# Which engine waits for the last landings: from SyncE to GpSimd, without GpSimd's drain

## The chip, the cores and the metric

The kernel runs on one core of one Trainium2 chip. The time is device microseconds of one execution. A core has five engines that work side by side, each with its own queue of instructions: TensorE (PE in the profile), VectorE (DVE), ScalarE (ACT), GpSimd (POOL) and SyncE (SP). They meet only through semaphores: an instruction can wait until a semaphore has a value, and can step one when it is done. Transfers are issued from an engine's queue, run on 16 DMA engines, and step a semaphore by 16 in all when they have landed.

## The reference

Eight experts, each a layer of two matrix products with a ReLU between them, on its own 256 rows:

```python
# x: 8 x 256 x 512, w1: 8 x 512 x 2048, w2: 8 x 2048 x 512, all float32
h = np.matmul(x, w1)
h = np.maximum(h, 0)
return np.matmul(h, w2).astype(np.float32)
```

## The kernel before

The weights make up most of the bytes. They are loaded from GpSimd's queue (`load_w1`, `load_w2`, lines 130 to 139), which turns float32 into bfloat16 on the way, into two buffers each, one for even and one for odd experts. The first half of `x` comes by SyncE's queue as float32 and is cast by VectorE and ScalarE, the second half by GpSimd's queue. TensorE transposes `x` by an identity matrix, then works through the experts in pairs: the first layer of both experts of a pair (line 269), then the second layer of both (line 289). VectorE takes one half of each result out of PSUM and ScalarE the other (`layers`, lines 202 to 226), with the ReLU behind the first layer (lines 216 and 218) and as a plain copy into `o_sb` behind the second (line 225).

The output leaves in three stores. GpSimd, when it has issued its last loads and the first four experts are copied, stores these (line 165, semaphore `s_out[0]`). SyncE stores experts 4 to 6 (line 125, `s_out[1]`) and, when the last copy is done, expert 7 (line 127, `s_out[2]`). GpSimd's queue carries the loads and its store in the order of their issue, so that store moves behind the last weights. Everything that GpSimd has to do for the kernel is issued by line 165; behind it stands a drain (line 166), an instruction that ends when the engine has finished what was given to it. SyncE's list is a long row of waits that hand landings on to TensorE, then the two stores, and at the end of the program, at line 300, the waits for all three stores:

```python
    for s in s_out:
        sp.wait_ge(s, 16)
```

The framework's own closing is taken early (`tc.close()`, line 97), so the kernel ends in these waits, and behind them in whatever every program on this chip has behind its last instruction.

Of the kernel before, what the change touches and what calls it, by code (L numbers as in the profile page):

```python
# [9 lines left out]
def kernel(  # L10
# [73 lines left out]
    sp, pool, act, dve, pe = nc.sync, nc.gpsimd, nc.scalar, nc.vector, nc.tensor  # L84
# [78 lines left out]
            load_w2(e + b)  # L163
    copied(pool, G)
    pool.dma_start(out_r[:, :G], o_sb[:, :G]).then_inc(s_out[0], 16)
    pool.drain()

# [127 lines left out]
                        ins.then_inc((s_ob, s_oa)[m], 1)  # L297

    for s in s_out:
        sp.wait_ge(s, 16)  # L300


# [28 lines left out]
```

## Time and profile before

| | |
|---|---|
| time, median of 3 runs | 179.96 us (179.84 to 180.02) |
| the profiled execution, its own time | 179.85 us |
| its span, first to last instruction of the program | 178.5 us |
| TensorE busy | 130.2 us, 73% of the span |
| VectorE, ScalarE busy | 37.2 and 37.8 us |
| GpSimd busy | 12.6 us |
| GpSimd's DMA queue (q0) | 36.70 MB, 94.2% of the 16 engines' time |
| the hardware queue (q1) | 4.19 MB, 6.0% |
| mean granted TensorE clock | 0.963 |

How to read it: the profile is of one execution. The span counts only the program's own instructions; the time of an execution is longer, since something lies around them. Waiting, branching and issuing are not counted as busy time, so SyncE, which does nothing else, has no row among the busy engines; its waits have a view of their own. A drain counts as a sequencer instruction too and shows only in the view of its line. In the DMA issues, the last column is the time from issue to landing. In the lines of the timeline, the columns are start and duration in us, engine, line, operation, what it writes and reads, and in brackets the idle time before it with what ended that. A trailing q on an engine's name (SPq, POOLq) means its sequencer.

### The profile page before, as it was taken

What the parts mean: (1) busy time and instruction counts of PE and PEld (TensorE: products, weight loads), DVE (VectorE), ACT (ScalarE), POOL (GpSimd) and SP (SyncE); (2) the same over time, 40 slices, a digit from 0 to 9 for tenths busy, and PEclk for the clock granted to TensorE, in tenths of its full rate; (3) what the DMA queues carried; (4) which work ended last, traced back from release to release, by engine and by line L of the source; (5) the groups of instructions that cost most, each with busy time, mean ns of one, the idle gap of its engine ahead of it and who ended that gap; (6) DMA issues with size and microseconds to landing.
All of it is one profiled execution on the core that took longest, in us unless ns stands there. A gap on an engine that the chain in (4) does not pass through costs nothing. (4 is left out here: it accounts for less than half of the span.)

```text
span 178.5 us, 2361 instructions
## 1 busy us (share of the span) xinstructions
PE 130.2 (73%) x824; PEld 89.1 (50%) x832; DVE 37.2 (21%) x48; ACT 37.8 (21%) x49; POOL 12.6 (7%) x26
## 2 busy tenths in 40 slices
PE   0235299796949697899769398969496695998950
PEld 0224189693413296785333287954142694953410
DVE  0333673331010133131101033320101141311010
ACT  2464763221010122121100022220101121311010
POOL 3600000101010101001000101010201200000000
PEclk9999999999987999699999789999999999999996
DMA  5999999989989989999999998999998999999998
GB/s 195 350 218 235 217 195 235 224 191 231 231 191 224 235 191 220 235 202 209 235 209 202 235 224 187 235 228 195 224 235 191 220 235 194 207 224 209 269 423 353
DMA packets 4384, 40.90 MB, mean 229 GB/s; under 512 B 416, under 2 KB 416, under 8 KB 2208
## 3 DMA queue, kind: packets, MB, share of 16 engines
q0 software_dynamic: 3264, 36.70, 94.2%
q1 hardware_dynamic: 1120, 4.19, 6.0%
HBM read 71.30 MB, written 4.19 MB: 423 GB/s over the span
## 5 line engine op out<-in xcount | busy, mean ns | idle before, releaser
L269 PE MATMUL pt_h<-xe,w_sb 128*128 x512 | 65.4, 285 | 13.7 <-PEq L87 13.6
L269 PEld LDWEIGHTS pt_h<-xe,w_sb 128*128 x512 | 57.6, 147 | 22.0 <-issue 20.0
L289 PE MATMUL pt_o<-w_sb,ht_sb 128*128 x248 | 57.8, 387 | 11.8 <-PEq L87 11.4
L289 PEld LDWEIGHTS pt_o<-w_sb,ht_sb 128*128 x256 | 24.9, 99 | 43.4 <-issue 15.9
L218 DVE TENSOR_SCALAR ht_sb<-pt_h 128x512 bf16<-128x512 f32 x32 | 22.1, 692 | 52.9 <-PE pt_h L269 52.9
L216 ACT ACTIVATE ht_sb<-pt_h 128x512 bf16<-128x512 f32 x32 | 19.1, 597 | 57.9 <-PE pt_h L269 57.9
L253 PE MATMUL pt_tr<-identity,x_b 128*128 128x128 bf16 x64 | 7.5, 310 | 16.4 <-PEq L87 16.4
L225 DVE COPY out_sb<-pt_o 128x512 f32 x8 | 5.5, 692 | 66.5 <-PE pt_o L289 66.5
L225 ACT COPY out_sb<-pt_o 128x512 f32 x8 | 4.7, 586 | 64.6 <-PE pt_o L289 64.6
L253 PEld LDWEIGHTS pt_tr<-identity,x_b 128*128 128x128 bf16 x64 | 6.5, 144 | 17.1 <-issue 17.1
L131 POOL DMA_DIRECT2D w_sb<-in_w_dram x8 | 4.3, 534 | 70.9 <-ACTq L220 70.9
L195 DVE COPY xe<-pt_tr 128x1024 bf16<-128x1024 bf16 x2 | 4.9, 2454 | 5.2 <-PE pt_tr L253 5.2
L195 ACT COPY xe<-pt_tr 128x1024 bf16<-128x1024 bf16 x2 | 4.9, 2469 | 4.1 <-PE pt_tr L253 4.1
L136 POOL DMA_DIRECT2D w_sb<-in_w_dram x6 | 3.2, 536 | 35.5 <-ACT out_sb L225 35.5
L176 ACT CAST x_b<-x_f 128x1024 bf16<-128x1024 f32 x2 | 4.0, 2008 | 1.3 <-DMA x_f<-in_x_dram 1.3
L176 DVE CAST x_b<-x_f 128x1024 bf16<-128x1024 f32 x2 | 2.2, 1079 | 6.0 <-DMA x_f<-in_x_dram 6.0
L192 ACT COPY xe<-pt_tr 128x1024 bf16<-128x1024 bf16 x2 | 2.0, 1012 | 4.1 <-PE pt_tr L253 4.1
L192 DVE COPY xe<-pt_tr 128x1024 bf16<-128x1024 bf16 x2 | 1.4, 692 | 4.8 <-PE pt_tr L253 4.8
L138 POOL DMA_DIRECT2D w_sb<-in_w_dram x2 | 1.1, 531 | 17.1 <-ACT out_sb L225 17.1
L176 ACT COPY x_b<-x_c 128x1024 bf16<-128x1024 bf16 x2 | 2.2, 1119 | 0.0
L176 ACT ACT_TABLE_LOAD x1 | 1.3, 1283 | 2.9 <-PEq L98 2.9
L176 DVE COPY x_b<-x_c 128x1024 bf16<-128x1024 bf16 x2 | 1.4, 696 | 0.0
(9 smaller groups left out, 4.4 us busy)
## 6 DMA issues: line engine op xcount, KB each, us to landing
w_sb<-in_w_dram POOLq DMA_DIRECT2D x14, 2048.0 KB, 29.8
w_sb<-in_w_dram POOLq DMA_DIRECT2D x2, 1152.0 KB, 26.4
x_f<-in_x_dram SPq DMA_DIRECT2D x4, 512.0 KB, 4.1
out_dram<-out_sb POOLq DMA_DIRECT2D x1, 2048.0 KB, 35.9
w_sb<-in_w_dram POOLq DMA_DIRECT2D x2, 896.0 KB, 30.2
out_dram<-out_sb SPq DMA_DIRECT2D x1, 1536.0 KB, 8.6
x_c<-in_x_dram POOLq DMA_DIRECT2D x1, 1024.0 KB, 9.8
out_dram<-out_sb SPq DMA_DIRECT2D x1, 512.0 KB, 5.8
```

What stands on the lines that cost most here:

```text
L131: pool.dma_start(w1_k[:, e % 2 * KT1:(e % 2 + 1) * KT1], w1_r[e]).then_inc(s_w1[e], 16)
L136: pool.dma_start(w2_k[:, k:k + KT2], w2_r[e]).then_inc(s_w2[e], 16)
L138: pool.dma_start(w2_k[:, k:k + CUT], w2_r[e, :, :CUT]).then_inc(s_w2[e], 16)
L176: copy(x_b[:, b].rearrange("p (t m) q -> p t m q", m=MT), src.rearrange("p m (q t) -> p t m q", t=KT1),).then_inc(t_xb, 1)
L192: copy(xe[:, a * n:(a + 1) * n], pt[b][:].rearrange("p j q -> p (j q)")).then_inc(s_xe[b], 1)
L195: copy(xl[:, :, :, :, a - G].rearrange("p l j q -> p j l q"), pt[b][:].rearrange("p j (l q) -> p j l q", l=G),).then_inc(s_xe[b], 1)
L216: act.activation(dst, ph[half][:], relu).then_inc(t_h, 1)
L218: dve.tensor_relu(dst, ph[half][:]).then_inc(t_h, 1)
L225: copy(outs[b], po[:, half]).then_inc(s_copied, 1)
L253: ins = pe.transpose(pt[b][:, j], x_b[:, b, j], identity[:])
L269: ins = pe.matmul(ph[i // 2][:, i % 2, :], ws[i % 2 * KT1 + kt], xs[kt], start=(kt == 0), stop=(kt == KT1 - 1),)
L289: ins = pe.matmul(po[:, m], hs[(kt - k0) * MT + m], ws[kt - k0], start=(kt == 0), stop=(kt == KT2 - 1),)
```

## The change

The drain behind GpSimd's store goes, and the three waits at the program's end are put on GpSimd's queue in place of SyncE's. The stores, their queues and their semaphores stay as they are. GpSimd comes to these waits after its store is issued; SyncE has nothing behind its store of expert 7.

```diff
     copied(pool, G)
     pool.dma_start(out_r[:, :G], o_sb[:, :G]).then_inc(s_out[0], 16)
-    pool.drain()
...
     for s in s_out:
-        sp.wait_ge(s, 16)
+        pool.wait_ge(s, 16)
```

## The prediction

> **What bounds the kernel now.** I read the page first (busy shares and slices), then SyncE's waits, the timeline of the last ten microseconds, the DMA issues, and the two lines that the change touches.
>
> ```profile
> PE 130.2 (73%) x824; PEld 89.1 (50%) x832; DVE 37.2 (21%) x48; ACT 37.8 (21%) x49; POOL 12.6 (7%) x26
> ...
> DMA  5999999989989989999999998999998999999998
> ...
> q0 software_dynamic: 3264, 36.70, 94.2%
> q1 hardware_dynamic: 1120, 4.19, 6.0%
> ```
>
> The 16 DMA engines are busy nine tenths or more in nearly every slice, TensorE 73%: the kernel is bound by its transfers, weights first and the output last. 94.2% of that time is GpSimd's queue (the casting loads), and the change touches none of its issues. So I look at the end alone.
>
> ```profile
> 157.13 7.07 PE L289 MATMUL pt_o<-w_sb,ht_sb 128*128 x31
> ...
> 164.99 7.07 PE L289 MATMUL pt_o<-w_sb,ht_sb 128*128 x31 [0.79 <-PEq L87]
> 168.62 0.40 SPq L125 DMA_DIRECT2D out_dram<-out_sb  x1
> 171.88 0.69 DVE L225 COPY out_sb<-pt_o 128x512 f32 x1 [7.17 <-PE pt_o L289]
> 172.10 0.59 ACT L225 COPY out_sb<-pt_o 128x512 f32 x1 [7.27 <-PE pt_o L289]
> 172.71 0.35 SPq L127 DMA_DIRECT2D out_dram<-out_sb  x1
> ```
>
> ```profile
> out_dram<-out_sb POOLq DMA_DIRECT2D x1, 2048.0 KB, 35.9
> ...
> out_dram<-out_sb SPq DMA_DIRECT2D x1, 1536.0 KB, 8.6
> ...
> out_dram<-out_sb SPq DMA_DIRECT2D x1, 512.0 KB, 5.8
> ```
>
> ```profile
> 138.60 0.77 POOL L165 DMA_DIRECT2D out_dram<-out_sb  x1
> ```
>
> TensorE ends at 164.99 + 7.07 = 172.06, VectorE's last copy at 172.57, ScalarE's at 172.69. Then only stores are under way: GpSimd's lands at 138.60 + 35.9 = 174.5, SyncE's at 168.62 + 8.6 = 177.2 and 172.71 + 5.8 = 178.5, which is the end of the span.
>
> ```profile
> SPq L300 <- DMA out_dram<-out_sb: 5.4, 2, 4.2
> ```
>
> ```profile
> L300 SPq EVENT_SEMAPHORE  x2: 17/22/28, 177.3 to 178.5; - x2
> ```
>
> ```profile
> L166 POOLq DRAIN  x1: 36787/36787/36787, 138.5 to 138.5; - x1
> ```
>
> SyncE stands 5.4 us at line 300 and its last wait (28 ns, starting at 178.5) is the program's last instruction. GpSimd's drain lasts 36.787 us from 138.5, so it ends at 175.3: 0.9 us behind the landing of GpSimd's store and 3.2 us ahead of the span's end. **So the removed drain is off the path by 3.2 us, and the time of the landings is set by the transfers.** What is left to change is which engine sees the last landing, and what comes behind that.
>
> **What comes behind the span.** The profiled execution took 179.85 us with a span of 178.5 us, so 1.3 us lie around the program's instructions. No row of the views shows them, but the trace also holds the time of each semaphore update, and semaphore 2, which the program never uses, is stepped there. These are its updates from 172 us on, and the last of the 16 landing updates of some transfers (us from the span's start; the rows are the trace's own list, put in lines by me):
>
> ```
> semaphore 2, first round:   172.237 172.801 175.857 175.901 178.668 178.712 178.750 178.784 178.833
> semaphore 2, second round:  179.622 179.656 179.694 179.738 179.762 179.860 179.898 179.933 179.979
> all other semaphores:       one update each, between 178.796 and 179.398
> ends of instructions:        GpSimd's drain 175.322, SyncE's last wait 178.543
> s_out, last landing update: s_out[0] 174.450   s_out[1] 177.252   s_out[2] 178.498
> weights, last update:       s_w1[5] 109.983  s_w2[4] 119.727  s_w2[5] 129.393  s_w1[6] 139.041
>                             s_w1[7] 148.724  s_w2b[6] 158.496  s_w2b[7] 168.472
> startup: semaphore 96 stepped at 2.181, GpSimd's wait on it begins at 2.205;
>          semaphore 97 stepped at 2.719, SyncE's wait on it begins at 2.735
> ```
>
> I read semaphore 2 as a barrier that passes through the five engines, up and back down: nine updates in each round, hops of 34, 38, 44 and 24 ns up in the second round, 98, 38, 35 and 46 ns back. In the first round each engine posts only when it has finished. 172.237 is 0.18 us behind TensorE's last matmul, 172.801 is 0.12 behind ScalarE's last copy, 175.857 can only be GpSimd (0.535 behind its drain's end at 175.322), 175.901 follows it by one hop (VectorE, long done), and 178.668 is SyncE, 0.125 behind its last wait's end at 178.543. So the order is TensorE, ScalarE, GpSimd, VectorE, SyncE; then the round goes back down, the semaphores are cleared, and a second round ends at 179.98. All of this lies in a chain behind SyncE's post at 178.668, so the time moves by as much as that post moves.
>
> **The change part by part.**
>
> *The drain goes.* One instruction of 36.787 us, nothing of the kernel queued behind it on GpSimd (the store of line 165 is issued ahead of it), its end covered by SyncE's wait for 3.2 us. Removing it gains nothing in the span: 0.
>
> *SyncE's wait goes.* SyncE is free at 172.71 + 0.35 = 173.06 and waits in the barrier behind VectorE. It no longer needs its 0.125 us between wait and post; it posts one hop after VectorE.
>
> *GpSimd waits.* From about 139.4 on it stands in the three waits; behind them on its queue is nothing of the kernel, so the body (loads, casts, matmuls, copies) is unchanged. It sees the last landing (178.498) as late as SyncE or a little later. The trace has no GpSimd wait on a landing. The nearest row is the start-up one above: GpSimd's wait begins 24 ns behind the step that releases it, SyncE's 16 ns; that makes +0.01 us. The far bound is a GpSimd instruction that has to be started by software:
>
> ```profile
> 136.68 0.59 ACT L225 COPY out_sb<-pt_o 128x512 f32 x1 [9.09 <-PE pt_o L289]
> 137.56 0.53 POOL L138 DMA_DIRECT2D w_sb<-in_w_dram  x1 [8.62 <-ACT out_sb L225]
> ```
>
> ScalarE's copy ends at 137.27 and the DMA instruction starts at 137.56, 0.29 us on. A plain wait is like the first, so I take +0.01 us, bounds 0 and +0.27. A gain is excluded here: the landing itself cannot be seen before it happens, and SyncE reacted within 0.05 us.
>
> *GpSimd's step from its last instruction to its post.* This is the term that decides. Before, it took 0.535 us (175.322 to 175.857) and was hidden in SyncE's 3.2 us. Now it begins where the last wait ends, at 178.543 + 0.01 = 178.553, and nothing hides it: GpSimd posts at 179.088. For an end behind a wait in place of a drain the bounds are 0.125 (as SyncE's, were the 0.535 a matter of the drain) and 0.535 + 0.87 (were the drain's work, 174.450 to 175.322, done behind the last wait). I take 0.535, the only row of this engine.
>
> *The hops that follow.* GpSimd stands third of five, SyncE was the top. Behind GpSimd's post VectorE needs 44 ns (175.857 to 175.901) and SyncE 24 ns (179.738 to 179.762): 0.068 us. SyncE's post falls at 179.156 in place of 178.668. The Trainium skill, "Runtime: NRT & Kernel Launch", section "The ~15µs preamble/postamble breakdown", gives 44 ns for each hop; by it the two hops would be 0.088 us and the sum 0.02 higher, an estimate. The trace's own hops run from 24 to 98 ns, so the rows are used.
>
> *Sum:* 0.01 + (0.535 - 0.125) + 0.068 = +0.49 us. Against the profiled execution 179.85 + 0.49 = 180.34; the median of the runs shown stands 0.11 above that execution, so 179.96 + 0.49 = **180.45 us**, 0.27% slower. What a measurement of this kernel can tell from no change is about 0.2%, that is 0.36 us, so the forecast lies just beyond it.
>
> **The rivals.**
>
> *The closing step costs GpSimd no more than SyncE (not slower).* If the 0.535 us come from the drain itself (the time for an engine that was flushed to go on), a GpSimd that ends in a plain wait posts 0.125 us behind it, and only the wait's 0.01 and the 0.068 of hops are left: 179.96 + 0.08 = 180.04, within 0.2%. It decides as soon as the step is under about 0.41 us. For it: ScalarE, TensorE and SyncE all post 0.12 to 0.18 us behind their last instruction. Against it: a drain is meant to leave nothing behind, and the trace shows no reason why the next instructions should be late. The same page of the Trainium skill, same section, lists what the runtime puts behind a kernel as stages of fixed time; by that rule it would not matter which engine is last, and the result would be this rival's. The trace does not bear it out in full, since the step differs by engine (0.535 against 0.125). Chance 0.19.
>
> *The drain's work is moved, not saved (slower still).* The drain ended 0.87 us behind the landing it waited for. If GpSimd's closing has to do the same once its last wait ends, the step is 0.535 + 0.87: 179.96 + 0.49 + 0.87 = 181.32. For it: 0.87 us is long for an instruction whose condition is met. Against it: at 178.5 that store is 4 us old, so whatever follows a landing has had its time. Chance 0.15.
>
> *The drain holds up the transfers (faster).* While GpSimd drains, its loads might run slower. The unbroken load under the drain landed 148.724 - 139.041 = 9.683 us behind the one ahead of it, as 129.393 - 119.727 = 9.666 without it; but the two that are cut in two took 9.772 and 9.976, together 0.42 us more than two of 9.666. If the drain and not the cut is the cause, 0.42 us come back, and with a closing as cheap as in the first rival the time is 179.96 - 0.42 + 0.08 = 179.62, at the edge of what counts as faster; I count it there. It decides where it takes back more than the closing costs. Against it stands the unbroken load, and that the store's own packets run beside the last of these loads. Chance 0.09.
>
> **How the numbers follow.** Forecast 0.57, cheap closing 0.19, moved drain 0.15, freed transfers 0.09. The range is to leave out no more than 0.2: from 179.95 (the cheap closing less 0.09 for the spread of the runs, which reach from 179.84 to 180.02) to 180.95 (the forecast with the wait's far bound, 180.71, and the lower part of the moved drain); freed transfers and the upper part of the moved drain stay out. The forecast alone has 180.2 to 180.7. Slower: 0.57 + 0.15, less 0.04 for a step a little under 0.41, is 0.68. Same: 0.19 + 0.04 = 0.23. Faster: 0.09.
>
> **What the changed profile would show.** No drain on GpSimd; GpSimd's wait ending at 178.5 as the span's last instruction, so a span within 0.1 us of 178.5; the loads' landings unmoved; and 1.8 us in place of 1.3 us between span and time. In the list of semaphore 2: GpSimd's post 0.5 us behind the span's end, VectorE's and SyncE's directly behind it. A post at 0.13 us makes the first rival right, one at 1.4 us the second, an earlier last landing the third. A span that grows by 0.2 us or more would say that GpSimd sees a landing late, and then the wait's price was mis-sized.

## The result, and the profile after

The changed kernel takes 180.78 us (median of 6 runs, 180.30 to 181.16); the kernel before took 179.92 us (6 runs, 179.84 to 180.04) beside it. The ratio is put at 1.0036, 95% interval 1.0019 to 1.0052 (it is not the quotient of the two medians, which is 1.0048): slower, and the interval leaves out no change. The profiled execution took 180.30 us with a span of 178.5 us.

The page's busy times, its DMA slices and its two queues stand nearly as before (TensorE 131.6 us busy for 130.2, the others within 1%):

```profile
PE 131.6 (74%) x824; PEld 89.8 (50%) x832; DVE 37.2 (21%) x48; ACT 37.7 (21%) x49; POOL 12.6 (7%) x26
...
DMA  5999989989989989989998998998998999999998
...
q0 software_dynamic: 3264, 36.70, 94.3%
q1 hardware_dynamic: 1120, 4.19, 6.0%
```

The end of the changed kernel in the timeline (start and duration in us, engine, line, operation):

```profile
165.03 7.07 PE L288 MATMUL pt_o<-w_sb,ht_sb 128*128 x31 [0.79 <-PEq L87]
168.52 0.40 SPq L125 DMA_DIRECT2D out_dram<-out_sb  x1
171.91 0.69 DVE L224 COPY out_sb<-pt_o 128x512 f32 x1 [7.16 <-PE pt_o L288]
172.13 0.58 ACT L224 COPY out_sb<-pt_o 128x512 f32 x1 [7.27 <-PE pt_o L288]
172.74 0.35 SPq L127 DMA_DIRECT2D out_dram<-out_sb  x1
```

Its DMA issues (KB, and us from issue to landing), and the line of the waits, now on GpSimd (durations of one in ns, then first and last start):

```profile
out_dram<-out_sb POOLq DMA_DIRECT2D x1, 2048.0 KB, 35.7
...
out_dram<-out_sb SPq DMA_DIRECT2D x1, 1536.0 KB, 8.6
...
out_dram<-out_sb SPq DMA_DIRECT2D x1, 512.0 KB, 5.7
```

```profile
L299 POOLq EVENT_SEMAPHORE  x2: 17/30/43, 177.2 to 178.4; - x2
```

SyncE's own waits (total us, times, longest) no longer have a row for the stores' landings; the largest that are left are the waits for weights and copies:

```profile
SPq L115 <- DMA w_sb<-in_w_dram: 86.5, 8, 19.2
SPq L120 <- DMA w_sb<-in_w_dram: 34.7, 6, 9.7
SPq L102 <- DVE out_sb L224: 33.1, 5, 7.7
SPq L123 <- DMA w_sb<-in_w_dram: 7.7, 2, 4.2
SPq L122 <- DMA w_sb<-in_w_dram: 5.5, 1, 5.5
```

At this end nothing of the program has moved by more than about 0.1 us: TensorE ends at 172.10 (172.06 before), the last store goes out at 172.74 (172.71) and lands after 5.7 us (5.8). The last instruction is GpSimd's wait, 43 ns from 178.4. The span ends at 178.461 (178.543), and yet the execution is 0.45 us longer than the profiled one before. So the time came from behind the span. The trace's list of semaphore 2 shows it (us from the span's start):

```
before:   span's end 178.543
  first round    172.237 172.801 175.857 175.901 178.668 178.712 178.750 178.784 178.833
  second round   179.622 179.656 179.694 179.738 179.762 179.860 179.898 179.933 179.979
changed:  span's end 178.461
  first round    172.273 172.834 178.992 179.035 179.059 179.156 179.196 179.230 179.277
  second round   180.073 180.107 180.145 180.189 180.213 180.311 180.349 180.384 180.430
```

The third post, GpSimd's, has gone from 175.857 to 178.992, 0.531 us behind the end of its last wait; VectorE and SyncE, both long ready, follow 43 and 24 ns later. The last update lies 1.969 us behind the span's end where it lay 1.436 behind: **+0.533 us**. The runs say the same without the trace: time less span was 1.80 to 1.88 us in the six runs, 1.85 in the median, where the profiled execution before has 1.31.

The medians differ by 0.86 us, 0.3 more than this. That part is the span, which scatters from one execution to the next: 178.5 to 179.3 us in these six runs. The experiments below show that the kernel before scatters as widely.

### The profile page after: what moved, and what is told of

It reads as the page before. It is cut to its first block, busy times and chain, and to the rows that moved or that the text cites. A ratio compares the mean times of both kernels' runs of the same rounds, so it can differ in the third digit from the quotient of the medians.

```text
span 178.5 us, 2360 instructions
## 1 busy us (share of the span) xinstructions
PE 131.6 (74%) x824; PEld 89.8 (50%) x832; DVE 37.2 (21%) x48; ACT 37.7 (21%) x49; POOL 12.6 (7%) x26
## 5 line engine op out<-in xcount | busy, mean ns | idle before, releaser
L268 PE MATMUL pt_h<-xe,w_sb 128*128 x512 | 66.8, 289 | 13.6 <-PEq L87 13.5
L268 PEld LDWEIGHTS pt_h<-xe,w_sb 128*128 x512 | 58.4, 147 | 22.6 <-issue 19.9
```

What stands on the lines that cost most here:

```text
L268: ins = pe.matmul(ph[i // 2][:, i % 2, :], ws[i % 2 * KT1 + kt], xs[kt], start=(kt == 0), stop=(kt == KT1 - 1),)
```

## The experiments

I held that GpSimd's own step between its last instruction and its post is the price, whatever that last instruction is, and that SyncE had been hiding it (theory A in the texts on record). Against it stood that a drain is owed at the end and comes back, that the price belongs to the wait, and that the missing drain lengthens the span of some executions (theory B). Four kernels were timed beside the kernel before on the same chip and at the same time, whose own median there was 180.40 us (29 runs, 179.75 to 181.30, spans from 178.4 to 180.0, time less span 1.26 to 1.40, median 1.32); the other six were run once each and are read by their trace. The times that were expected of the four with spans of 178.5 to 178.7 us turned out 0.42 to 0.53 us too low; the kernel before itself stood 0.44 higher than in the prediction (180.40 for 179.96). So the effects are read from time less span, and from the medians beside one another.

**The drain alone is removed.**

```diff
-    pool.drain()
```

> SyncE waits as before, only the drain is gone. Theory A (GpSimd's own closing step of 0.53 us is exposed because GpSimd ends last): GpSimd's step is hidden again, time less span 1.31 us, spans within 178.5 to 178.7, time 179.9 us, within 0.1 us of before. Theory B (a missing drain lengthens some executions, by up to 0.8 us of span): time less span 1.31 us, but spans scattered from 178.5 to 179.3 and a median of about 180.25 us.

```profile
L299 SPq EVENT_SEMAPHORE  x2: 17/22/28, 177.2 to 178.5; - x2
```

180.32 us (12 runs, 179.70 to 181.61) for 180.40 beside it, ratio 1.0015, interval 0.9995 to 1.0034: no difference that can be told. Time less span: 1.31 us in the median, as before. In the trace SyncE posts 0.124 us behind its last wait, and GpSimd, with no drain, has posted long ago, at 172.982, one hop behind ScalarE. The drain itself cost nothing, as its 3.2 us of cover said. Its spans go from 178.4 to 180.3 us, but the kernel before, which has its drain, scattered as widely beside it (178.4 to 180.0), so the scatter isn't the missing drain's. Theory A's 1.31 us is met, and its spans of 178.5 to 178.7 us are missed. Theory B's numbers, scattered spans and a time of about 180.25 us, are nearly met, but its cause is not: the kernel that has the drain shows the same, with a median span of 179.1 us for 179.05 here.

**The waits alone are moved.**

```diff
     for s in s_out:
-        sp.wait_ge(s, 16)
+        pool.wait_ge(s, 16)
```

> GpSimd waits at the end, but keeps its drain ahead of the waits. Theory A: GpSimd posts 0.53 us behind its last wait all the same, time less span 1.84 us, 180.45 us with spans of 178.5 to 178.7. If the step came from a drain that is still owed, it is shorter here: time less span under 1.5 us. Theory B: the scatter of the spans is gone, since the drain is back (median 180.45); if the scatter comes from GpSimd's waits at the end, spans reach 179.3 and the median is about 180.8.

180.90 us (12 runs, 180.21 to 181.83), ratio 1.0033, interval 1.0011 to 1.0054. Time less span: 1.84 us in the median. The lines of the drain and of the waits:

```profile
L166 POOLq DRAIN  x1: 35187/35187/35187, 140.6 to 140.6; - x1
```

```profile
L300 POOLq EVENT_SEMAPHORE  x2: 17/30/42, 177.7 to 179.0; - x2
```

The expected 180.45 us is missed, and the spans reach from 178.4 to 180.0, just as with the kernel before. The drain ends at 175.75, 3.2 us ahead of the last wait, and GpSimd's step behind that wait is 0.538 us all the same (178.996 to 179.534). The whole price belongs to the moved wait, and having drained earlier doesn't shorten the step.

**The changed kernel once more.**

> The changed kernel once more, unchanged, for the scatter of its span. Time less span 1.84 us in each run by theory A. Theory B and the theory that the waits lengthen the span: spans again from 178.5 to 179.3, median 180.8 us. If the scatter belonged to the occasion, spans stay at 178.5 to 178.7 and the median is 180.45 us.

```profile
L299 POOLq EVENT_SEMAPHORE  x2: 17/30/43, 177.7 to 178.9; - x2
```

180.98 us (6 runs, 180.82 to 181.22), ratio 1.0049, interval 1.0030 to 1.0068; time less span 1.83 us in the median; spans 179.0 to 179.4, within what the kernel before spread over. Against the median beside it that is 0.58 us, close to the 0.53 us of the trace; the 0.86 us of the first comparison held 0.3 us of scatter. The step in the trace: 0.531 us.

**ScalarE waits** (GpSimd keeps its drain; the same edit with `act.`).

> ScalarE waits at the end in place of SyncE, GpSimd keeps its drain. Theory A with the barrier's order (TensorE, ScalarE, GpSimd, VectorE, SyncE) gives: ScalarE's step 0.12 us, hops of 38, 44 and 24 ns to SyncE and 98 ns back to VectorE, so VectorE's second post falls 0.32 us behind the span's end where before it fell 0.17 behind: time less span 1.46 us, time about 180.07 us. If any engine but SyncE paid 0.5 us, time less span would be 1.84 us and the time 180.45 us.

```profile
L300 ACTq EVENT_SEMAPHORE  x2: 17/28/38, 177.7 to 179.0; - x2
```

180.59 us (12 runs, 179.99 to 181.65), ratio 1.0021, interval 1.0002 to 1.0040. Time less span 1.46 us in the median, as computed. The trace: ScalarE's step is 0.114 us (179.013 to 179.127), the three hops up to SyncE 38, 44 and 24 ns, the way back to VectorE 97 ns; the last update lies 1.586 us behind the span's end, 0.150 more than with SyncE. So the cost of ending last differs by engine. ScalarE's step is no longer than SyncE's; what it costs more is its earlier place in the barrier.

**VectorE waits, and TensorE waits** (the same edit with `dve.` and with `pe.`).

> VectorE waits at the end in place of SyncE, GpSimd keeps its drain. From the barrier's order (TensorE, ScalarE, GpSimd, VectorE, SyncE): VectorE's step about 0.12 us, one hop of 24 ns up to SyncE, then 98 ns back to VectorE and 38, 34, 46 ns on. The second round of semaphore 2 then ends 1.51 us behind the span's end, 0.07 us more than with SyncE (1.436). If VectorE's step is as long as GpSimd's (0.53 us), it ends 1.92 us behind.

> TensorE waits at the end in place of SyncE, GpSimd keeps its drain. TensorE stands first in the barrier, so all four hops up (34, 38, 44, 24 ns) lie behind its post. With a step of 0.12 to 0.18 us the second round of semaphore 2 ends 1.62 to 1.68 us behind the span's end, 0.18 to 0.25 us more than with SyncE (1.436). With a step like GpSimd's (0.53 us) it would end 2.04 us behind.

The waits' lines, of VectorE and of TensorE (whose waits are on the sequencer of its weight loads):

```profile
L300 DVEq EVENT_SEMAPHORE  x2: 21/36/50, 177.7 to 178.9; - x2
```

```profile
L300 PEldq EVENT_SEMAPHORE  x2: 51/51/51, 178.1 to 179.3; - x2
```

With VectorE its step is 0.140 us (178.992 to 179.132) and the last update lies 1.530 us behind the span's end (1.51 expected). With TensorE the step is 0.193 us (179.364 to 179.557) and the last update lies 1.694 us behind, just past the 1.62 to 1.68 expected, since the step is longer by 0.013 than I had bounded it. TensorE's trace has the clearest picture of a barrier in which all others are ready, nine updates with about the hops of the second round:

```
179.557 179.591 179.630 179.674 179.697 179.796 179.835 179.869 179.916
```

No engine but GpSimd takes 0.5 us. SyncE, which stands last on the way up, remains the cheapest: of the five I found no order that beats the kernel before.

**GpSimd waits for its own store alone.**

```diff
-    pool.drain()
+    pool.wait_ge(s_out[0], 16)
...
-    for s in s_out:
+    for s in s_out[1:]:
         sp.wait_ge(s, 16)
```

> GpSimd waits for its own store alone, in place of its drain; SyncE waits for its two stores. GpSimd's wait ends at about 174.4 us, its post comes at about 174.9, 3.6 us ahead of SyncE's, and hides. The second round of semaphore 2 ends 1.436 us behind the span's end, as before: no change. If GpSimd's closing step were longer whenever it ends in a wait, it would still hide up to 3.6 us, so anything above 1.5 us here would say that not GpSimd being last, but GpSimd waiting at all is the price.

```profile
L166 POOLq EVENT_SEMAPHORE  x1: 17/17/17, 174.8 to 174.8; - x1
```

GpSimd's wait ends at 174.863, it posts at 175.394, 0.531 us on, and SyncE's post comes at 178.992. The last update lies 1.433 us behind the span's end, as with SyncE alone. GpSimd may end in a wait; what costs is to be last.

**GpSimd's drain behind the waits** (the changed kernel with a drain as its last instruction).

```diff
     for s in s_out:
         pool.wait_ge(s, 16)
+    pool.drain()
```

> As the changed kernel, with GpSimd's drain put behind its three waits. If the 0.87 us that the drain took behind its store's landing are work that a drain always does, the drain lasts 0.8 to 0.9 us here, the span is 179.4 us or longer by that much than the landing, and the time less span stays at 1.84 us. If they are over once the landing is some us old, the drain lasts under 0.2 us and the whole costs under 0.2 us more than the changed kernel.

```profile
L300 POOLq DRAIN  x1: 1682/1682/1682, 178.9 to 178.9; - x1
```

Neither answer that I had written down: the drain takes 1.682 us, 4 us behind the landing of GpSimd's store. The span becomes 180.551 us and the execution took 182.42. The step behind the drain is 0.528 us, so the work of the drain stands in the drain, and the closing is neither longer nor shorter for it. The prediction's second rival had that work in the closing; it isn't there.

**Two drains, and a drain behind the landing but ahead of SyncE's end.** The first keeps the drain of line 166, moves the waits to GpSimd and drains once more behind them; the second waits for GpSimd's own store, drains, and leaves the other waits with SyncE.

> GpSimd keeps its drain behind its store, waits for the landings at the end and drains once more behind them. If the 1.68 us of the drain placed last were work owed for the transfers issued since the start, the first drain has done it and the second takes under 0.1 us (34 to 65 ns at start-up): the second round of semaphore 2 ends about 2.0 us behind the last wait's end. If any drain at that place takes 1.68 us, it ends about 3.7 us behind it.

> GpSimd waits for its own store, then drains; SyncE waits for its two stores. If a drain that begins behind the landings takes 1.68 us, GpSimd's ends at about 174.5 + 1.7 = 176.2 and its post falls at 176.7, still 1.8 us ahead of SyncE's: hidden, and the second round of semaphore 2 ends 1.436 us behind the span's end. If the time behind a landing is 0.87 us as in the kernel before, the drain lasts about 0.87 us, hidden as well.

The two drains of the first kernel, then the one of the second:

```profile
L166 POOLq DRAIN  x1: 36349/36349/36349, 139.6 to 139.6; - x1
```

```profile
L301 POOLq DRAIN  x1: 47/47/47, 179.4 to 179.4; - x1
```

```profile
L167 POOLq DRAIN  x1: 1690/1690/1690, 174.6 to 174.6; - x1
```

The second drain takes 47 ns, so the 1.68 us are work that the first drain does and the next need not do again. That it is owed for the transfers that GpSimd has issued is my reading; no run varied their number. The last update lies 181.373 - 179.315 = 2.06 us behind the last wait's end. In the other kernel the drain takes 1.690 us though its store has just landed, ends at 176.271, GpSimd posts at 176.801, 0.530 us on, and all of it is hidden: 1.434 us from the span's end to the last update.

All twelve traces together (the step is from the end of the engine's last instruction to its post):

```
kernel                            last engine  its step   span's end to last update of semaphore 2
before                            SyncE        0.125 us   1.436 us
drain removed                     SyncE        0.124      1.437
GpSimd waits for its own store    SyncE        0.119      1.433
drain late, hidden                SyncE        0.120      1.434
VectorE waits                     VectorE      0.140      1.530
ScalarE waits                     ScalarE      0.114      1.586
TensorE waits                     TensorE      0.193      1.694
changed                           GpSimd       0.531      1.969
changed, once more                GpSimd       0.531      1.966
waits moved, drain kept           GpSimd       0.538      1.973
waits moved, two drains           GpSimd       0.530      1.968
changed, drain behind the waits   GpSimd       0.528      1.998
```

## Why the prediction was right

*The body and the removed drain: right.* 0 was forecast for both. The landings and the last stores are where they were to about 0.1 us, and the kernel with the drain alone removed can't be told from the one before. One trace speaks for the prediction's reading that the transfers set the last landing: with the waits moved and the drain kept, TensorE ended at 174.16 us, 1.6 us later than in the other three traces with spans of 179.0 us, and the last store still landed at 178.93 us, as it did there (178.91 to 178.95).

*GpSimd's step: right.* 0.535 us were taken from the one row that there was, behind a drain; behind a wait it is 0.531, and between 0.528 and 0.538 in all nine traces that show it, drained or not, waiting or draining. The first rival (0.125 us) and the second (0.535 + 0.87) both fall here. What follows the last instruction has no fixed length in this case: 1.43 to 2.00 us by the engine that ends last. The Trainium skill, "Runtime: NRT & Kernel Launch", section "The ~15µs preamble/postamble breakdown", gives one approximate time for each stage behind a kernel; that this makes the length the same whichever engine ends last was my reading, and the traces do not bear it out. My argument against the second rival was wrong all the same: I held that 4 us behind a landing whatever follows it has had its time, and a drain placed there took 1.68 us. The rival falls because GpSimd's closing does not contain that work.

*The hops: right, but a turn was left out.* 0.068 us were forecast from GpSimd's post to SyncE's, and 0.067 measured. But I let the way back start from SyncE's post as before. VectorE, which has only just posted, takes 97 ns to answer SyncE, where it took 44 when it had been waiting: +0.053. So the step of the prediction by which the time moves by as much as SyncE's post was short by this. The rows for this stood in the prediction (98 ns on the way back in the second round, 44 in the first) and I had not asked why they differ.

*The wait: right in size.* GpSimd's last wait ends 67 ns behind the last landing update (178.394 to 178.461) where SyncE's ended 45 ns behind it: +0.022 for a forecast of +0.01, far from its upper bound of 0.27. It begins 24 ns behind the update, just as the start-up row had it; what I had not counted is that the wait itself lasts 43 ns where SyncE's lasts 28.

*The sum:* 0.49 us forecast with the wait's 0.01 in it. Behind the span, 0.406 from the step, 0.067 from the hops, 0.053 from the turn and 0.007 from the clearing between the two rounds are 0.533 measured, and 0.02 for the wait come on top: 0.555 us for the whole change.

*The time: in the range, in part by luck.* 180.45 was forecast, 180.78 measured. The prediction gave 180.2 to 180.7 for its forecast alone, and 180.78 lies above that; the room up to 180.95 came from the wait's far bound and the second rival, and neither happened. What used it is the scatter of the span, for which I had allowed 0.09 us at the lower end and nothing above. The remaining 0.3 us are no term of the change: time less span is 1.83 to 1.85 us in the median of each set of runs in which GpSimd ended last, and the spans of the kernel before cover the same stretch beside the experiments. I had read the spread of a kernel from three runs (179.84 to 180.02), which was too narrow by far: the kernel before later spread over 1.5 us. Its two sets of runs have medians of 179.92 and 180.40 us, further apart than the 0.36 us that I had called the least that a measurement can tell. Where that comes from was not tried; the traces show part of it already in the first weights, which landed at 22.80 us in the profile before and at 23.35 in that of the changed kernel run once more; the spans of these two profiles are 178.5 and 179.0.

*The third rival* (a drain that holds up the transfers) falls with the loads that ran while the drain stood open: the unbroken one, and the two behind it that are cut in two. Without the drain the unbroken load takes 9.683 us as with it (139.219 to 148.902). The first of the two cut ones takes 9.776 us without it and 9.772 with it (148.902 to 158.678 without). The second took 9.976 with the drain and 9.775 without (158.678 to 168.453), which alone would speak for the rival, but it scatters: over all traces it took 9.69 to 10.23 us where a drain stood at line 166 and 9.76 to 9.98 where none did. The 0.1 us by which the first takes longer than the unbroken load is there with and without the drain. In two of the six traces with that drain, though, one of the first two loads took 0.13 to 0.14 us more (9.826 for the unbroken one, 9.901 for the first cut one), in none of the six without; whether the drain has a part in that is open.

## What to carry to other kernels

The end of the program is not the end of the time: look at what each engine still does behind its last instruction, and let the engine for which that is shortest wait for the last landing. Here that is SyncE, and GpSimd as the last engine costs 0.53 us more. In single times this is hard to see, since the spans of one and the same kernel spread over 1.5 us; time less span, or the trace behind the last instruction, shows it at once. An engine with a long closing should finish some us earlier, where others hide it: GpSimd's 0.53 us cost nothing behind its own store. Drains belong early for the same reason: the same drain was free under a wait of 3.2 us and cost 1.7 us behind it.

## What the runs showed of the hardware that I had not expected

A drain on GpSimd that begins when its transfers have all landed still takes 1.68 to 1.69 us, and 47 ns when another drain went ahead of it; one that begins while they are under way ends 0.86 to 0.87 us behind the last landing (174.450 to 175.322 before, 174.883 to 175.746 with the waits moved). Whether that grows with the number of transfers was not tried.

GpSimd's 0.53 us between its last instruction and its post are the same behind a drain, a wait and two drains, and no row of the profile names what they are. That they belong to GpSimd as such, and not to its having issued transfers, was not tried either; SyncE, which issued six transfers by the hardware queue, takes 0.125 us.
